# Closing pairs with their first product ahead: B21's transfers issued by GpSimd, three within the product with S4, the fourth behind the first addition

## The chip, the cores and the metric

The kernel runs on one core of a Trainium2 chip. The metric is the device time of one execution in microseconds (us), lower is better. Several executions of a kernel are timed and their median is quoted; one further execution is recorded by the profiler.

The engines are named as in the profile: PE (TensorE, matrix products), PEld (its weight loads), DVE (VectorE), ACT (ScalarE), POOL (GpSimd) and SP (SyncE, which here does nothing but issue transfers). Transfers run on queues of their own; SP, ACT and POOL issue them, each into its own queue.

## The reference

A bidirectional encoder layer on 512 positions of width 2048, all in float32. Cut to what matters here:

```python
h = rmsnorm(x, norm_w)
u = h @ w_in            # z_ssm, xBC, dt, q_a, kv_a, z_attn, g_ssm, g_attn are its column blocks
...                     # branch A: conv, SSD scan in both directions, gated RMSNorm -> y (512 x 2048)
...                     # branch B: latent attention, gated -> o (512 x 2048)
merged = jax.nn.sigmoid(g_ssm) * (y @ w_proj_ssm) + jax.nn.sigmoid(g_attn) * (o @ w_proj_attn)
return rmsnorm(x + merged @ w_out, final_norm_w)
```

The change lies in one product of this, `y @ w_proj_ssm` with its gate: a 512 x 2048 matrix by a 2048 x 2048 one.

## The kernel before

**Products.** A float32 product is made of three passes with rounded parts: every weight chunk of 128 x 1024 is split by `w_split` into a high part (`wh`, an ACT cast, L483) and a low part (`wl`, a DVE subtraction, L484), and PE runs high x high, low x high and high x low (L629, L630, L631). The left operands are split likewise, once each (`split`, the same lines).

**Strassen pairs.** The big products are not made directly: `Strassen.pair(cp)` computes one half of the output columns (cp is 0 or 1) by the Strassen-Winograd scheme, with seven products of quarter size, P1 to P7. Each is made by `product`: four weight chunks m = 0 to 3, each of 12 matmuls of 128 x 512, into two banks. Called A the left matrix and B the right one, the right operands are: B11 for P1, B21 for P2, T1 for P5, T2 = T1 + B22 for P6, B22 for P3, T3 for P7 and, last, T4 for P4, where T4 = T2 + B21. Left operands are x11, x12, x21, x22 and their sums S1 to S4. T1 lies in the tiles X[0] to X[3]; T2 is made in them by `t2`, and T4 by `t4` (L752, a DVE addition of one 128 x 1024 chunk, out X, in X and a raw chunk of B21). B22 lies in the tiles Y; P7's T3 is loaded later, into Y tiles again.

**The closing pairs of w_proj_ssm.** There P1 and P2 of both pairs are made early (`head`), while the attention part runs. So `pair(cp, True)`, run for cp = 0 and then cp = 1, starts with P5 and goes P5, P6, P3 (with S4), P7 (with S3), P4 (with x22). In the pairs that make P2 in their middle, B21 is at hand for `t4` as P2's weights. In the two headed pairs it isn't, and B21 is loaded a second time for T4: `t4_alone` (L754 to L757), called for m = 0 to 3 as P7 takes its chunk m, issues the load on SP's queue (L756) into a tile `wraw` and then the addition. After the pairs of w_proj_ssm come those of w_proj_attn.

**Buffers and hooks.** The tag `wraw` has three buffers of 128 x 1024 in all. In this stage they hold raw halves of left operands (`xraw`, loaded on SP, two for each operand, split later by ACT and DVE) and the B21 chunks of `t4_alone`. Hooks place the work on left operands: at the end of P5 of pair 0, S4 is split and S3 is loaded; at P3's chunk m = 2 (`P3a`), S3 is split and x22 is loaded; at P7's chunk m = 3 (`P7a`), x22 is split. For pair 1 there are others of the kind.

**POOL's queue.** POOL computes nothing here; it issues transfers: loads of gate chunks (`fetch_ps`, L1503, tile `gate`), stores of finished output blocks (`done_ps`, L1513, into `ms_d`), and sums of the next left operands by copies and accumulating copies from DRAM to DRAM (`o_S<-o_x`, `o_S<-o_S`, L1456 and L1459). A transfer that waits holds back those behind it on the issuing engine.

**What sets the order.** PE's order is the order of the code. DVE, ACT, POOL and SP are ordered by a scheduler from priorities; `high_priority(offset=...)` moves an instruction ahead, and `keep_in_program_order` binds it to the order of the code on its engine. Each engine then runs its instructions strictly in that fixed order: an instruction that waits holds those behind it. The scheduler also decides which buffer a tile gets, and with it whose end a load has to wait for.

Of the kernel before, what the change touches and what calls it, by code (L numbers as in the profile page):

```python
# [73 lines left out]
def build(tc, a):  # L74
    nc = tc.nc
    act, dve, pool, pe = nc.scalar, nc.vector, nc.gpsimd, nc.tensor
# [440 lines left out]
    def w_load(t, w, cp, kh, cb, m):  # L517
        with tc.high_priority(offset=LOAD_AHEAD):
            nc.sync.dma_start(t, a[w][cp, kh, cb, m])
        return t  # L520

    def t_load(t, w, cp, name, m, queue=nc.sync):
        with tc.high_priority(offset=LOAD_AHEAD):
            queue.dma_start(t, t_d[w, cp, name][:, m * 1024:(m + 1) * 1024])
        return t
# [27 lines left out]
    def w_more(t, w, cp, kh, cb, m, ahead_=AHEAD):  # L553

        with tc.high_priority(offset=ahead_):
            pool.dma_start(t, a[w][cp, kh, cb, m], accum_op=ALU.add)
# [11 lines left out]
    def col_tile(tag, name, dt=F32):  # L568

        if tag == "Y" and cols is xb:  # L570
            n_cols[0] += 1
            return cols.tile([P, 1024], dt, tag=("Yb", "Ya")[(n_cols[0] - 1) // 2 % 2], bufs=2, name=name)
        return cols.tile([P, 1024], dt, tag=tag, bufs=4, name=name)

    def w_tile(tag):
        with tc.high_priority(offset=LOAD_AHEAD):
            if tag == "w":
                return wp.tile([P, 1024], F32, tag="wraw", bufs=3, name="wraw")
            return col_tile(tag, tag)

    def sum_tile(tag):

        if tag == "kk" or tag == "u" and kk:
            return kk.tile([P, SEQ], F32, tag="kk", bufs=2, name=tag)
        return part_.tile([P, SEQ], F32, tag=tag, bufs=2, name=tag)

    def evict(banks, tag, tile_=None):
        out = []
        with tc.high_priority(offset=AHEAD):
            for i, b in enumerate(banks):  # L590
                out.append(tile_(tag, i) if tile_ else sum_tile(tag))
                act.copy(out[-1], b)
        return out
# [19 lines left out]
    def product(name, op, chunk, extra=None, pre=None):  # L613

        used.append((used[-1] + 1) % 4)
        bs = [b(name) for b in SETS[used[-1]]]
        for m in range(4):
            raw = chunk(m)
            h, l = w_split(raw)
            if extra:  # L620
                extra(m, raw)
            if pre and m == 2:
                pre()
            for i in range(2):
                for jj in range(2):
                    j = 2 * m + jj
                    xh, xl = op(0, j, i), op(1, j, i)
                    wh, wl = (t[:, jj * 512:(jj + 1) * 512] for t in (h, l))
                    pe.matmul(bs[i], xh, wh, start=(j == 0), stop=False)  # L629
                    pe.matmul(bs[i], xh, wl, start=False, stop=False)  # L630
                    pe.matmul(bs[i], xl, wh, start=False, stop=(j == 7))  # L631
                    yield 3
        product_done()
        return bs
# [19 lines left out]
    class Strassen:  # L654
# [60 lines left out]
        def pair(self, cp, headed=False):  # L715
            w, made = self.w, self.made
            X, Y = self.ahead.pop(cp, []), []

            def column(m):
                if m == len(X):  # L720
                    X.append(self.columns(w_tile("X"), cp, m))
                return X[m]

            if headed:
                p1 = self.p1[cp]
            else:
                p1 = evict((yield from product(
                    "P1", self.op("x11"), (lambda m: w_load(w_tile("X"), w, cp, 0, 0, m)) if made else column,
                    None if made else lambda m, raw: w_more(raw, w, cp, 0, 1, m))), "p1", self.tile_)
                self.hook(cp, "P1")  # L730

            def c5(m):
                if m == 1:
                    self.hook(cp, "P5a")
                column(m)
                Y.append(w_load(w_tile("Y"), w, cp, 1, 1, m))
                return X[m]

            T3 = []

            def c7(m):
                if made and not T3:
                    T3.extend(t_load(w_tile("Y"), w, cp, "T3", i) for i in range(4))
                return T3[m] if made else Y[m]

            def t2(m, raw):
                with tc.high_priority(offset=AHEAD):
                    dve.tensor_add(raw, raw, Y[m])

            def t4(m, raw):  # L750
                with tc.high_priority(offset=AHEAD):
                    dve.tensor_add(X[m], X[m], raw)  # L752

            def t4_alone(m, raw):  # L754
                raw = w_tile("w")
                tc.keep_in_program_order(nc.sync.dma_start(raw, a[w][cp, 1, 0, m]))  # L756
                t4(m, raw)  # L757

            p5 = evict((yield from product("P5", self.op("S1"), c5, t2)), "p5", self.tile_)
            self.hook(cp, "P5")  # L760
            A = yield from product("P6", self.op("S2"), lambda m: X[m])
            u = p1 if headed else [self.tile_("u", i) for i in range(2)]
            for i in range(2):
                dve.tensor_add(u[i], p1[i], A[i])
                self.minus_r(p5[i], p5[i], u[i])
            self.hook(cp, "P6")
            if not headed:
                yield from self.second(cp, p1, lambda i: p1[i], t4)
                self.hook(cp, "P2")
            def more(m, raw):  # L770
                if not made:
                    w_more(raw, w, cp, 0, 1, m)
                if m == 2:
                    self.hook(cp, "P3a")

            B = yield from product("P3", self.op("S4"), lambda m: Y[m], more, self.pre(0, 2 * cp + 1))
            for i in range(2):
                o = sum_tile("ms") if headed else self.tile_("C12" if self.last else "p1", i)
                self.r_sum(o, p5[i], B[i])
                self.done(i, 2 * cp + 1, o)  # L780
            self.hook(cp, "P3")
            def late(m, raw):
                if headed:
                    t4_alone(m, raw)
                if m == 3:
                    self.hook(cp, "P7a")

            A = yield from product("P7", self.op("S3"), c7, late, self.pre(2, 2 * cp + 1))
            for i in range(2):
                self.minus_r(p5[i], p5[i], A[i])  # L790
                self.done(2 + i, 2 * cp + 1, p5[i])
                dve.tensor_add(u[i], u[i], A[i])
            self.hook(cp, "P7")
            if self.last:
                yield from self.last("P4", self.op("x22"), lambda m: X[m], u)
                return
            A = yield from product("P4", self.op("x22"), lambda m: X[m], None, self.pre(2, 2 * cp))
            for i in range(2):
                self.r_sum(u[i], u[i], A[i])
                self.done(2 + i, 2 * cp, u[i])  # L800
            self.hook(cp, "P4")
# [1118 lines left out]
```

## Time and profile before

| what | us |
|---|---|
| median of 3 runs (1955.85 to 1956.60) | 1956.28 |
| the profiled execution, its own time | 1956.44 |
| its span | 1954.6 |
| PE busy in the span | 1931.2 |
| DVE busy | 1464.2 |
| ACT busy | 1039.0 |

The span runs from the first to the last instruction of the program; the execution's own time is 1.8 us longer. Times within the span are counted from its start. The stage of the change lies between 1507 and 1621: pair 0 runs P5 from 1506.8, P6 from 1518.0, P3 from 1529.2, P7 from 1540.0 and P4 from 1550.9; pair 1 runs P5 from 1564.4, P6 from 1575.3, P3 from 1586.2, P7 from 1597.1 and P4 from 1609.4; the first product of w_proj_attn starts at 1621.1. The view that compares stretches of time, asked for pair 0, pair 1 and the 56 us behind them, reads (columns: stretch, its length, busy us of each engine with its instructions, granted clock, share of the DMA engines, GB/s):

```profile
1507.00:1564.00 57.00, 54.92 (x239) 44.20 (x238) 50.24 (x53) 27.00 (x28) 7.81 (x14) 1.00 0.80 259
1564.00:1621.00 57.00, 55.54 (x243) 45.15 (x242) 50.68 (x54) 29.45 (x30) 10.98 (x19) 1.00 0.84 282
1621.00:1677.00 56.00, 55.25 (x240) 44.52 (x240) 50.52 (x51) 29.14 (x31) 3.77 (x7) 1.00 0.71 251
```

DVE is busy for 50 of 57 us here, and the DMA engines for 80% and more of the time: nearer to full than in the mean of the kernel.

In the rows of the profile and of the order, names are cut: P is the bank pair of the product that runs, `S__13413` the operand S4, `S__13530` S3, `x__13657` x22, `x__13934` x12 of the attention side, `S__14022` its S1; `p`, `kk`, `ms` are 128 x 512 output blocks.

### The profile page before, as it was taken

What the parts mean: (1) busy time and instruction counts of PE and PEld (TensorE: products, weight loads), DVE (VectorE), ACT (ScalarE), POOL (GpSimd) and SP (SyncE); (2) the same over time, 40 slices, a digit from 0 to 9 for tenths busy, and PEclk for the clock granted to TensorE, in tenths of its full rate; (3) what the DMA queues carried; (4) which work ended last, traced back from release to release, by engine and by line L of the source; (5) the groups of instructions that cost most, each with busy time, mean ns of one, the idle gap of its engine ahead of it and who ended that gap; (6) DMA issues with size and microseconds to landing.
All of it is one profiled execution on the core that took longest, in us unless ns stands there. A gap on an engine that the chain in (4) does not pass through costs nothing.

```text
span 1954.6 us, 24595 instructions
## 1 busy us (share of the span) xinstructions
PE 1931.2 (99%) x8873; PEld 1590.9 (81%) x8874; DVE 1464.2 (75%) x2064; ACT 1039.0 (53%) x1536; POOL 252.8 (13%) x324
## 2 busy tenths in 40 slices
PE   8999999999999999999999999999999999999998
PEld 6878888888888888888888888888888777888886
DVE  7876676766759869789786557676777898879467
ACT  7444444444465866757757444444455455454344
POOL 0011001001112030030210211111011110100011
PEclk9999999999999999999999999999999999999999
DMA  6569669668554545665554867787388887847447
GB/s 219 174 191 260 161 169 248 151 184 242 144 190 153 180 147 158 214 193 179 177 161 147 231 191 208 205 219 201 101 220 303 277 261 279 285 156 243 162 89 170
DMA packets 145306, 383.29 MB, mean 196 GB/s; under 512 B 16608, under 2 KB 34208, under 8 KB 144992
## 3 DMA queue, kind: packets, MB, share of 16 engines
q1 hardware_dynamic: 78240, 232.45, 35.7%
q0 software_dynamic: 31392, 105.40, 23.8%
q10 hardware_dynamic: 35552, 43.87, 6.3%
q8 instruction: 70, 1.15, 0.2%
q14 instruction: 52, 0.43, 0.1%
HBM read 329.55 MB, written 98.17 MB: 219 GB/s over the span
## 4 chain that ended last, share of the span: by engine, by line
PE 48%; DVE 3%; DMA 2%; issue 1%; ACT 0%; SPq 0%; DVEq 0%; ACTq 0%
PE P L630 5%; PE P L631 4%; PE P L629 4%; PE za L169 3%; PE za L171 3%; PE za L170 3%; PE f L1678 1%; PE f L1679 1%; PE f L1680 1%; PE pb L1431 1%; PE qp L171 1%; PE qp L169 1%; PE qp L170 1%; DMA wraw<-wps 1%; DVE wl L484 1%; PE s L1409 1%
## 5 line engine op out<-in xcount | busy, mean ns | idle before, releaser
L483 ACT CAST wh<-X 128x1024 fp32r<-128x1024 f32 x164 | 172.7, 1055 | 198.9 <-PE P L631 156.0
L484 DVE TENSOR_TENSOR wl<-X,wh 128x1024 fp32r<-128x1024 f32 x164 | 199.9, 1223 | 87.0 <-ACT wh L483 86.5
L165 DVE TENSOR_TENSOR wl<-wraw,wh 128x1024 fp32r<-128x1024 f32 (+2 forms) x148 | 173.1, 1172 | 79.8 <-ACT wh L164 74.5
L164 ACT CAST wh<-wraw 128x1024 fp32r<-128x1024 f32 (+2 forms) x148 | 142.8, 969 | 112.6 <-PE za L170 29.0
L484 DVE TENSOR_TENSOR wl<-Y,wh 128x1024 fp32r<-128x1024 f32 x88 | 107.6, 1224 | 71.8 <-ACT wh L483 71.8
L483 ACT CAST wh<-Y 128x1024 fp32r<-128x1024 f32 x88 | 93.0, 1057 | 117.9 <-PE P L631 107.3
L169 PE MATMUL xbc<-h_h,wh 128*128 128x512 f32 x384 | 153.1, 399 | 0.0
L171 PE MATMUL xbc<-h_h,wl 128*128 128x512 f32 x384 | 149.9, 390 | 0.0
L170 PE MATMUL xbc<-h_l,wh 128*128 128x512 f32 x384 | 149.5, 389 | 0.0
L629 PE MATMUL P<-wh,h_h 128*128 128x512 f32 x384 | 149.4, 389 | 0.0
L630 PE MATMUL P<-wl,h_h 128*128 128x512 f32 x384 | 149.4, 389 | 0.0
L631 PE MATMUL P<-wh,h_l 128*128 128x512 f32 x384 | 149.4, 389 | 0.0
L483 ACT CAST wh<-wraw 128x1024 fp32r<-128x1024 f32 x68 | 71.8, 1056 | 115.7 <-PE P L631 63.4
L484 DVE TENSOR_TENSOR wl<-wraw,wh 128x1024 fp32r<-128x1024 f32 x68 | 83.2, 1223 | 60.3 <-ACT wh L483 60.3
L630 PE MATMUL P<-wl,S 128*128 128x512 f32 x288 | 112.4, 390 | 1.4 <-DVE wl L484 1.4
L631 PE MATMUL P<-wh,S 128*128 128x512 f32 x288 | 112.1, 389 | 0.0
L629 PE MATMUL P<-wh,S 128*128 128x512 f32 x288 | 112.1, 389 | 0.0
L169 PE MATMUL za<-h_h,wh 128*128 128x512 f32 x256 | 101.7, 397 | 0.0
L171 PE MATMUL za<-h_h,wl 128*128 128x512 f32 x256 | 100.0, 391 | 0.0
L170 PE MATMUL za<-h_l,wh 128*128 128x512 f32 x256 | 99.7, 389 | 0.0
L171 PEld LDWEIGHTS xbc<-h_h,wl 128*128 128x128 f32 x384 | 72.1, 188 | 15.6
L631 PEld LDWEIGHTS P<-wh,h_l 128*128 128x128 f32 x384 | 72.1, 188 | 15.0
(754 smaller groups left out, 5073.1 us busy)
## 6 DMA issues: line engine op xcount, KB each, us to landing
wraw<-wi SPq DMA_DIRECT2D x102, 512.0 KB, 3.8
T_wps<-wps POOLq DMA_DIRECT2D x32, 512.0 KB, 11.1
da<-da_d SPq DMA_DIRECT2D x64, 256.0 KB, 3.8
T_wpa<-wpa POOLq DMA_DIRECT2D x32, 512.0 KB, 9.7
wraw<-wps SPq DMA_DIRECT2D x24, 512.0 KB, 6.7
wraw<-wo SPq DMA_DIRECT2D x20, 512.0 KB, 3.5
xbc_d<-xbc ACTq DMA_DIRECT2D x24, 256.0 KB, 3.0
wraw<-wun SPq DMA_DIRECT2D x16, 384.0 KB, 6.0
```

Source lines behind the costliest of these rows:

```text
L164: act.copy(h, raw)
L165: dve.tensor_sub(l, raw, h.bitcast(F32))
L169: pe.matmul(out, wh, xh, start=start, stop=False)
L170: pe.matmul(out, wh, xl, start=False, stop=False)
L171: pe.matmul(out, wl, xh, start=False, stop=stop)
L483: i = act.copy(hi_, raw)
L484: dve.tensor_sub(lo_, raw, hi_.bitcast(F32))
L629: pe.matmul(bs[i], xh, wh, start=(j == 0), stop=False)
L630: pe.matmul(bs[i], xh, wl, start=False, stop=False)
L631: pe.matmul(bs[i], xl, wh, start=False, stop=(j == 7))
L1409: pe.matmul(s, qh[:, tk], kh, start=True, stop=False)
L1431: pe.transpose(tp[:, k * P:(k + 1) * P], prs[t][:, k * P:(k + 1) * P], ident)
```

## The change

The load of B21's chunk leaves `t4_alone` and becomes `b21_load`, which takes the next `wraw` tile and issues the load on POOL's queue instead of SP's, in program order there. In the headed pairs it is called three times in P3, at its chunks m = 0, 1 and 2 (at m = 2 ahead of the hook `P3a`), and a fourth time in P7, behind the addition of chunk 0. The additions stay in the code where they were, with priority `AHEAD`. The bytes, the matmuls and the arithmetic are the same. Below the change, lines behind L754 have numbers higher by 7, and those behind L772 by 9 (L1512 is L1521, for one).

```diff
+            b21 = []
+
+            def b21_load():
+                m = len(b21)
+                b21.append(w_tile("w"))
+                tc.keep_in_program_order(pool.dma_start(b21[m], a[w][cp, 1, 0, m]))
+
             def t4_alone(m, raw):
-                raw = w_tile("w")
-                tc.keep_in_program_order(nc.sync.dma_start(raw, a[w][cp, 1, 0, m]))
-                t4(m, raw)
+                t4(m, b21[m])
+                if m == 0:
+                    b21_load()
 ...
             def more(m, raw):
                 if not made:
                     w_more(raw, w, cp, 0, 1, m)
+                if headed and m < 3:
+                    b21_load()
                 if m == 2:
                     self.hook(cp, "P3a")
```

What the scheduler makes of it is seen in the order of the rows on DVE and POOL. First DVE in pair 0, from the end of P6 to the split of S3 (the operand `S__13530`, in the change `S__13536`); the first three `wl<-Y` are the low parts of P3's chunks 0, 1 and 2. Before:

```order
L484 TENSOR_TENSOR S__13413<-xraw,S__13413 128x1024
L484 TENSOR_TENSOR wl<-X,wh 128x1024
L484 TENSOR_TENSOR wl<-Y,wh 128x1024 x2
L764 TENSOR_TENSOR p_13002<-p_13002,P_13422 128x512
L764 TENSOR_TENSOR p_13004<-p_13004,P_13423 128x512
L676 TENSOR_TENSOR p_13409<-p_13409,p_13002 128x512
L484 TENSOR_TENSOR wl<-Y,wh 128x1024
L676 TENSOR_TENSOR p_13411<-p_13411,p_13004 128x512
L484 TENSOR_TENSOR S__13530<-xraw,S__13530 128x1024
```

Now:

```order
L484 TENSOR_TENSOR S__13413<-xraw,S__13413 128x1024
L484 TENSOR_TENSOR wl<-X,wh 128x1024
L484 TENSOR_TENSOR wl<-Y,wh 128x1024
L752 TENSOR_TENSOR X<-X,wraw 128x1024
L484 TENSOR_TENSOR wl<-Y,wh 128x1024
L771 TENSOR_TENSOR p_13002<-p_13002,P_13422 128x512
L771 TENSOR_TENSOR p_13004<-p_13004,P_13423 128x512
L676 TENSOR_TENSOR p_13409<-p_13409,p_13002 128x512
L484 TENSOR_TENSOR wl<-Y,wh 128x1024
L676 TENSOR_TENSOR p_13411<-p_13411,p_13004 128x512
L752 TENSOR_TENSOR X<-X,wraw 128x1024
L484 TENSOR_TENSOR wl<-Y,wh 128x1024
```

The first addition of T4 (L752) now stands ahead of the low part of P3's chunk 1, and the second ahead of that of chunk 3. Before, all four stood behind P3's splits. The third now stands ahead of the low part of P7's chunk 1 and the fourth ahead of that of P4's chunk 1.

The same place in pair 1, DVE, from P3's chunk 2 on; the last `wl<-Y` is P3's chunk 3. Before:

```order
L484 TENSOR_TENSOR wl<-Y,wh 128x1024
L676 TENSOR_TENSOR p_13850<-p_13850,kk 128x512
L676 TENSOR_TENSOR p_13852<-p_13852,kk 128x512
L484 TENSOR_TENSOR wl<-Y,wh 128x1024
L484 TENSOR_TENSOR S__14022<-xraw,S__14022 128x1024 x2
```

Now:

```order
L484 TENSOR_TENSOR wl<-Y,wh 128x1024
L676 TENSOR_TENSOR p_13850<-p_13850,kk 128x512
L676 TENSOR_TENSOR p_13852<-p_13852,kk 128x512
L752 TENSOR_TENSOR X<-X,wraw 128x1024
L484 TENSOR_TENSOR wl<-Y,wh 128x1024
L484 TENSOR_TENSOR S__14028<-xraw,S__14028 128x1024
```

Here the first addition stands ahead of the low part of P3's chunk 3; the second and third stand ahead of those of P7's chunks 1 and 2, the fourth ahead of that of P4's chunk 2.

POOL's queue in pair 0, from the DRAM sums to the stores of the blocks that P3 finishes. Before:

```order
L1459 DMA o_S_223<-o_x_219 128x512
L1459 DMA o_S_221<-o_x_220 128x512
L1503 DMA gate<-gs_d_1_154 128x512
L1513 DMA ms_d_1_178<-ms 128x512
L1503 DMA gate<-gs_d_1_158 128x512
L1513 DMA ms_d_1_182<-ms 128x512
L1503 DMA gate<-gs_d_0_153 128x512
```

Now:

```order
L1468 DMA o_S_223<-o_x_219 128x512
L1468 DMA o_S_221<-o_x_220 128x512
L1512 DMA gate<-gs_d_1_154 128x512
L759 DMA wraw<-wps 128x1024 x3
L1522 DMA ms_d_1_178<-ms 128x512
L1522 DMA ms_d_1_182<-ms 128x512
L759 DMA wraw<-wps 128x1024
L1512 DMA gate<-gs_d_1_158 128x512
L1512 DMA gate<-gs_d_0_153 128x512
```

Three loads stand behind the DRAM sums and a gate load, the fourth behind the stores. In pair 0 the scheduler gives the first load the buffer that the second raw half of S4 leaves, so it waits for that half's split on DVE; the second load gets the buffer of the first and waits for the first addition, the third that of the second and waits for the second addition. In pair 1 the first load stands on POOL behind the accumulating copy `o_S_224<-o_x_218` and waits for the second half of x12 (`x__13934`) to be split on DVE; the second waits for the first addition, the third and fourth get the buffers of S1's raw halves.

## The prediction

> **What bounds the kernel now.** The page's first part says which engine sets the time, and PE's timeline says where it loses any in the stage of the change.
>
> ```profile
> PE 1931.2 (99%) x8873; PEld 1590.9 (81%) x8874; DVE 1464.2 (75%) x2064; ACT 1039.0 (53%) x1536; POOL 252.8 (13%) x324
> ...
> 1534.81 0.39 PE L630 MATMUL P<-wl,S__13413 128*128 128x512 f32 x1
> 1535.04 0.39 PE L631 MATMUL P<-wh,S__13413 128*128 128x512 f32 x1
> ...
> 1556.12 0.39 PE L631 MATMUL P<-wh,x__13657 128*128 128x512 f32 x1
> 1557.26 0.49 PE L629 MATMUL P<-wh,x__13657 128*128 128x512 f32 x1 [0.75 <-ACT wh L483]
> 1559.08 0.50 PE L630 MATMUL P<-wl,x__13657 128*128 128x512 f32 x1 [1.32 <-DVE wl L484]
> 1559.41 0.40 PE L631 MATMUL P<-wh,x__13657 128*128 128x512 f32 x1
> ...
> 1602.50 0.39 PE L629 MATMUL P<-wh,S__13530 128*128 128x512 f32 x1
> 1603.91 0.50 PE L630 MATMUL P<-wl,S__13530 128*128 128x512 f32 x1 [1.02 <-DVE wl L484]
> 1604.25 0.40 PE L631 MATMUL P<-wh,S__13530 128*128 128x512 f32 x1
> ...
> 1609.43 0.39 PE L629 MATMUL P<-wh,x__13657 128*128 128x512 f32 x1
> 1610.25 0.50 PE L630 MATMUL P<-wl,x__13657 128*128 128x512 f32 x1 [0.44 <-DVE wl L484]
> 1610.59 0.39 PE L631 MATMUL P<-wh,x__13657 128*128 128x512 f32 x1
> ```
>
> PE is busy for 99% of the span, so the change can give only what PE waits for. Fed, a matmul starts 0.23 us after the one before (1534.81 to 1535.04); a chunk of 12 takes 2.72. Against that step, P4's chunk 2 in pair 0 loses 1.14 + 1.82 + 0.33 - 3 x 0.23 = 2.6 us. Pair 1 loses 1.41 + 0.34 - 0.46 = 1.3 in P7's chunk 2 and 0.82 + 0.34 - 0.46 = 0.7 in P4's chunk 0, together 2.0. The chain of work that ended last tells what these waited for:
>
> ```profile
> 1535.91 5.61 DMA wraw<-wps
> ...
> 1548.13 6.67 DMA wraw<-wps
> 1554.82 1.23 DVE X L752
> ...
> 1557.89 1.15 DVE wl L484
> ...
> 1592.81 6.93 DMA wraw<-wps
> ```
>
> All of it is B21: the load takes 6.7 us, the addition (L752) follows at once, then ACT's high and DVE's low part. Up to **4.6 us** are at stake in the two pairs. The execution took 1956.44 us, 0.16 above the median of the runs; I add to 1956.4. A measurement tells some 0.2% (3.9 us) from no change, so the whole gain would just be visible.
>
> **What the change moves.** It adds no instruction to PE and leaves DVE's additions at four per pair. The four loads leave SP, whose later loads move up; SP bounds nothing here. What counts is that the loads stand on POOL, and that the additions stand further ahead on DVE, in front of low parts that PE needs sooner. An addition that waits for its load holds the low part behind it. The rows for that, DVE first:
>
> ```profile
> 1522.22 1.23 DVE L484 TENSOR_TENSOR S__13413<-xraw,S__13413 128x1024 fp32r<-128x1024 f32 x1
> ...
> 1527.71 1.23 DVE L484 TENSOR_TENSOR wl<-Y,wh 128x1024 fp32r<-128x1024 f32 x1 [1.50 <-ACT wh L483]
> 1528.86 1.28 DVE L764 TENSOR_TENSOR p<-p,P 128x512 f32<-128x512 f32 x2
> ...
> 1541.54 1.23 DVE L752 TENSOR_TENSOR X<-X,wraw 128x1024 f32<-128x1024 f32 x1 [1.13 <-DMA wraw<-wps]
> 1542.69 1.22 DVE L484 TENSOR_TENSOR wl<-Y,wh 128x1024 fp32r<-128x1024 f32 x1
> ...
> 1557.80 2.36 DVE L484 TENSOR_TENSOR wl<-X,wh 128x1024 fp32r<-128x1024 f32 x2
> ...
> 1585.38 1.23 DVE L484 TENSOR_TENSOR x__13934<-xraw,x__13934 128x1024 fp32r<-128x1024 f32 x1 [1.41 <-ACT x__13934 L483]
> ```
>
> A load that lands at L frees the addition at L + 0.02 (1535.91 + 5.61 = 1541.52, start 1541.54). The low part starts 1.15 later, lasts 1.23, and PE's matmul with it starts 0.06 after (1557.80 + 1.22 = 1559.02, start 1559.08): **L + 2.46**. PE's own times for those matmuls, and the transfers nearest to the new loads (the issues' view, for windows around one or two of them; last column us to landing):
>
> ```profile
> 1532.09 0.39 PE L630 MATMUL P<-wl,S__13413 128*128 128x512 f32 x1
> ...
> 1553.85 0.39 PE L630 MATMUL P<-wl,x__13657 128*128 128x512 f32 x1
> ...
> 1594.57 0.39 PE L630 MATMUL P<-wl,S__13413 128*128 128x512 f32 x1
> ...
> 1523.52 0.33 SPq L495 DMA_DIRECT2D xraw<-yn_x  x1
> xraw<-yn_x SPq DMA_DIRECT2D x1, 512.0 KB, 8.0
> 1520.85 1.25 POOL L1503 DMA_DIRECT2D gate<-gs_d  x1
> o_S<-o_x POOLq DMA_DIRECT2D x1, 256.0 KB, 9.3
> gate<-gs_d POOLq DMA_DIRECT2D x1, 256.0 KB, 9.7
> 1587.65 0.86 POOL L1459 DMA_DIRECT2D o_S<-o_x  x1 [5.88 <-DMA o_S<-o_S]
> Y<-T_wps SPq DMA_DIRECT2D x1, 512.0 KB, 4.4
> o_S<-o_x POOLq DMA_DIRECT2D x1, 256.0 KB, 5.8
> 1542.80 0.33 SPq L756 DMA_DIRECT2D wraw<-wps  x1
> wraw<-wps SPq DMA_DIRECT2D x1, 512.0 KB, 4.0
> wraw<-wpa SPq DMA_DIRECT2D x1, 512.0 KB, 3.2
> ...
> 1546.13 0.55 POOL L1513 DMA_DIRECT2D ms_d<-ms  x1 [0.21 <-issue]
> ```
>
> **Pair 0, first load.** It may be issued when S4's second half is split, 1522.22 + 1.23 = 1523.5. Before, SP issues a load of the same size at that very moment (1523.52), and it takes 8.0, to 1531.5: two DRAM sums are under way. On POOL's queue the load stands behind a gate load that lands at 1520.85 + 9.7 = 1530.6; were it to begin only then, and alone, with 3.2 (the later load of w_proj_attn's weights), it would land at 1533.8. Transfers under way at one time overlap, so I take 1532.2, near the row of the same moment. PE's low pass of P3's chunk 1 then starts at 1532.2 + 2.46 = 1534.7 in place of 1532.09: **2.6 us lost**, from 1.9 to 4.2. Before, that low part was done at 1527.71 + 1.23 = 1528.9, 3.2 us early.
>
> **Pair 0, the rest.** Behind the first addition DVE has the low part of chunk 1 from 1533.4 (1.14 to the next, 2.36 - 1.22), three short sums of 0.6 (1.28 for two with the last one's end), the low part of chunk 2 (1.14), one sum more, and then the second addition. That is reached at 1533.4 + 1.14 + 1.8 + 1.14 + 0.6 = 1538.1, and its load, issued at 1533.4 into the buffer just freed, takes 4.0 to 5.6 (rows of `wraw` above): landed by 1537.4 to 1539.0. The low part of chunk 3 is then 0.3 to 1.2 late; I take 0.3. The third addition, ahead of P7's chunk 1, comes out 0 to 1 late: 0.2. The fourth load stands behind the two stores, which wait for P3's blocks (1546.13 before, some 4 us later now, for the low parts and additions moved ahead of them), and so lands at 1555 to 1557; P4's chunk 1 wants its low part at 1553.85 + 3.1, so L + 2.46 is 0.5 to 2.5 late: 0.8. Together **1.3**, from 0 to 4.5. In return the 2.6 of P4's chunk 2 go: the third addition is then some 10 us earlier than the 1554.82 of before. What is late next is P4's chunk 1, counted here. Pair 0: 2.6 + 1.3 - 2.6 = **+1.3**.
>
> **Pair 1, first load.** It waits for x12's second half (1585.38 + 1.23 = 1586.6), but stands on POOL behind the accumulating copy issued at 1587.65, which lands at 1593.5. A load on SP issued just after that copy took 4.4, to 1592.2: the lower bound. The upper is 1593.5 + 3.2 = 1596.7. I take 1594.6, nearer to the copy's row since that is of its queue. The low part behind the addition is P3's chunk 3, used at 1594.57: 1594.6 + 2.46 - 1594.57 = **2.5 lost**, from 0.1 to 4.6. Pair 0's delay moves both sides alike, because POOL's copies follow stores that wait for DVE.
>
> **Pair 1, the rest, and behind.** The second load follows the first addition (1595.8) and takes 4.0 to 6.9; P7's chunk 1 wants L + 2.46 by 1602.5: 0 to 2.7, I take 0.3. The fourth stands behind the stores again, ahead of P4's chunk 2: 1.0, from 0 to 3. The old losses of 2.0 go. Pair 1: 2.5 + 1.3 - 2.0 = **+1.8**. The loads of w_proj_attn's first chunks follow P4's splits and slip with them: +0.3, from -0.4 to 2.
>
> **Sum.** 1.3 + 1.8 + 0.3 = +3.4, so 1956.4 + 3.4 = **1959.8 us**. All low ends together give -4.6 + 1.9 + 0.1 - 0.4 = -3.0, or 1953.4; all high ends are near +16, but hold only if every transfer is late.
>
> **Rivals.** *It does what it says* (6%): the loads land before DVE comes to the additions, P3 is undisturbed and 4.6 us go: 1951.8. For it the first load of pair 0 has to land by 1532.09 - 2.46 = 1529.6, within 6.1 us of its issue, and that of pair 1 by 1592.1. For it speaks the 3.2 us of a load alone; against it the 8.0, 9.3 and 9.7 of that stretch. The Trainium skill, "DMA: Bandwidth & Descriptors", section "Anatomy of one DMA — SWDGE (gpsimd) path", fits a GpSimd transfer as 2.0 us plus its bytes at 436 GB/s, an estimate of 3.2 us for 512 KB; by that rule this rival would win. The trace differs: the gate load of half that size took 9.7. The same page, section "Queues, rings and completion order", has each DMA engine take the queues in turn and one queue's descriptors in order; by that the load would begin behind the gate load, near the upper bound of 1533.8, and pair 0 would lose some 1.6 us more.
>
> *Only pair 0 is held* (17%): in pair 1 the load overlaps with the copy and lands by 1592.2, and nothing else there is late. Then +1.3 - 2.0 + 0.3 = -0.4: 1956.0.
>
> *The additions form a chain* (25%): one buffer serves the first three loads of pair 0, so each is issued only after the addition before it. If each then takes 6 to 7 us, as B21's loads did in the rows of the chain, every addition holds its low part: pair 0 loses 4.2 + 4.0 - 2.6, pair 1 4.0 + 2.5 - 2.0, and w_proj_attn's start 1: near +11; with half of the terms late, +8. It decides where a load takes over 5 us on POOL. Against it speak the 4.0 us of the load at 1542.80 and the loads that the stalled DVE doesn't free yet, which leave the queues emptier. 1964.5 as its middle. This one is clearly slower.
>
> **How the numbers follow.** Forecast 52%, with its own range of 1957.5 to 1962; the rivals 6, 17 and 25. The range of 1955.0 to 1965.5 takes in the second rival and most of the chain and leaves out the first. Slower by over 0.2% (past 1960.2) is most of the chain and some two fifths of the forecast: 0.45. Within 0.2%: the rest of the forecast and all of the second rival, 0.5. Faster: 0.05.
>
> **What would show it.** In the profile after: the waits of PE at 1557.26, 1559.08, 1603.91 and 1610.25 are gone; DVE idles ahead of L752, released by `DMA wraw<-wps`, twice within P3, near 1532 and 1595, for 2 to 5 us; PE waits for `wl` at L630 with `S__13413` right behind. The `wraw` transfers of POOL take 5 to 9 us for each pair's first, 4 to 6 for the others. If PE has no wait with `S__13413`, the forecast is wrong and the first rival holds; if waits stand at three or more chunks of a pair with over 1 us each, it is the chain.

## The result, and the profile after

| | median of the runs | profiled execution | its span |
|---|---|---|---|
| before | 1955.85 us (5 runs, 1954.21 to 1956.60) | 1956.44 us | 1954.6 us |
| after | 1968.39 us (5 runs, 1967.62 to 1970.75) | 1968.39 us | 1966.6 us |

The ratio is 1.0068, with a 95% interval of 1.0056 to 1.0079: the change makes the kernel slower by 12.5 us. The forecast was 1959.8, its range ended at 1965.5. The side was right, the size was not.

PE's timeline of the changed kernel, at the six places where it loses time in the two pairs (a row: start, duration, engine, line, what it does, and in brackets the idle time with what ended it):

```profile
1530.46 0.39 PE L629 MATMUL P<-wh,S__13413 128*128 128x512 f32 x1
1533.17 0.71 PE L630 MATMUL P<-wl,S__13413 128*128 128x512 f32 x1 [2.33 <-DVE wl L484]
1533.68 0.63 PE L631 MATMUL P<-wh,S__13413 128*128 128x512 f32 x1
1534.11 0.63 PE L629 MATMUL P<-wh,S__13413 128*128 128x512 f32 x1
...
1547.03 0.50 PE L630 MATMUL P<-wl,S__13536 128*128 128x512 f32 x1 [1.07 <-DVE wl L484]
...
1557.82 0.39 PE L629 MATMUL P<-wh,x__13657 128*128 128x512 f32 x1
1561.01 0.80 PE L630 MATMUL P<-wl,x__13657 128*128 128x512 f32 x1 [2.80 <-DVE wl L484]
1561.60 0.63 PE L631 MATMUL P<-wh,x__13657 128*128 128x512 f32 x1
...
1602.12 0.50 PE L630 MATMUL P<-wl,S__13413 128*128 128x512 f32 x1 [1.36 <-DVE wl L484]
...
1611.60 0.50 PE L630 MATMUL P<-wl,S__13536 128*128 128x512 f32 x1 [0.72 <-DVE wl L484]
...
1622.43 0.39 PE L629 MATMUL P<-wh,x__13657 128*128 128x512 f32 x1
1626.96 0.80 PE L630 MATMUL P<-wl,x__13657 128*128 128x512 f32 x1 [4.14 <-DVE wl L484]
```

All six waits are for a low part. A wait is counted here as the step from one start to the next less the 0.23 us of a fed matmul: 2.5, 1.2, 3.0, 1.5, 0.9 and 4.3 us, together 13.4. Of the four places at which PE lost time before, three have no loss now. At the fourth, P7's chunk 2 in pair 1 (1603.91 before, 1611.60 now), PE still loses 0.9 us, now behind the third addition. Behind the 2.5 us wait something stands that the profile before has behind none of its waits: the matmuls last 0.63 instead of 0.39 and start 0.43 apart (1533.68 to 1534.11). The same holds behind the two waits in P4.

The first of the waits on DVE's timeline, what DVE waited for in the whole stretch (the view of waits: total, times, longest), and the chain of work that ended last in the second pair:

```profile
1523.58 1.23 DVE L484 TENSOR_TENSOR wl<-Y,wh 128x1024 fp32r<-128x1024 f32 x1 [0.45 <-ACT wh L483]
1530.76 1.23 DVE L752 TENSOR_TENSOR X<-X,wraw 128x1024 f32<-128x1024 f32 x1 [5.95 <-DMA wraw<-wps]
1531.90 1.22 DVE L484 TENSOR_TENSOR wl<-Y,wh 128x1024 fp32r<-128x1024 f32 x1
```

```profile
DVE X L752 <- DMA wraw<-wps: 22.2, 6, 6.6
```

```profile
1603.50 5.66 DMA wraw<-wps
...
1612.74 1.13 DVE wl L484
1613.88 0.61 DVE ms L1521
...
1615.99 8.53 DMA wraw<-wps
1624.54 1.23 DVE X L752
1625.77 1.15 DVE wl L484
1626.96 0.80 PE P L630
```

Both show the predicted mechanism: the load lands, the addition that DVE stood waiting at follows at once, then the low part behind it, then PE. The load that does most harm is the fourth. It is issued at 1615.99, behind a store that waited for the sum at 1613.88, and then takes 8.5 us.

The mean granted clock (PEclk) of stretches of 3.41 us, cut where the halved clock begins and ends in the trace (columns: the stretch, its length, busy time of PE, of its weight loads, of DVE, ACT and POOL with their instructions, PEclk, share of the DMA engines, GB/s):

```profile
1529.88:1533.29 3.41, 1.08 (x6) 0.58 (x5) 2.53 (x3) 1.95 (x3) 0.53 (x1) 1.00 0.11 44
1533.29:1536.70 3.41, 3.41 (x9) 2.64 (x10) 3.41 (x6) 0.00 (x0) 0.00 (x0) 0.50 0.89 294
1557.19:1560.60 3.41, 1.01 (x5) 0.51 (x3) 2.01 (x2) 0.68 (x1) 0.00 (x0) 1.00 0.98 382
1560.60:1564.01 3.41, 3.00 (x7) 2.43 (x8) 3.41 (x6) 0.37 (x1) 0.00 (x0) 0.50 1.00 359
1622.04:1625.45 3.41, 0.78 (x4) 0.32 (x2) 0.91 (x1) 0.00 (x0) 0.00 (x0) 1.00 1.03 420
1625.45:1628.87 3.42, 1.91 (x5) 1.53 (x6) 3.42 (x6) 2.00 (x2) 0.10 (x1) 0.50 0.92 340
```

A stretch in which PE does little is followed by one at half speed. It costs 25 matmuls about 0.2 us each (4.9 us), and 0.7 at the first steps behind the waits: 5.6 us.

### The profile page after: what moved, and what is told of

It is laid out like the page before. It is cut to its first block, busy times and chain, and to the rows that moved or that the text cites. A ratio compares the mean times of both kernels' runs of the same rounds, so it can differ in the third digit from the quotient of the medians.

```text
span 1966.6 us, 24608 instructions
## 1 busy us (share of the span) xinstructions
PE 1935.5 (98%) x8874; PEld 1595.3 (81%) x8874; DVE 1461.3 (74%) x2064; ACT 1037.4 (53%) x1536; POOL 256.5 (13%) x332
```

## The experiments

The theory at this point: **the additions' place** on DVE, in front of low parts, makes PE wait for whatever load is late; the fourth load is late because of its place on POOL; the half clock is a result of the waits. The main rival: GpSimd's queue is itself slow. A ratio is always to the kernel before, run beside it on the same chip.

**Other queue, other place of the additions, fourth load alone.** Three kernels, each the change with one edit:

```diff
 # x1_sp
-tc.keep_in_program_order(pool.dma_start(b21[m], a[w][cp, 1, 0, m]))
+tc.keep_in_program_order(nc.sync.dma_start(b21[m], a[w][cp, 1, 0, m]))
 # x2_add_behind
-t4(m, b21[m])
+tc.keep_in_program_order(dve.tensor_add(X[m], X[m], b21[m]))
 # x3_fourth_sp
-tc.keep_in_program_order(pool.dma_start(b21[m], a[w][cp, 1, 0, m]))
+tc.keep_in_program_order((nc.sync if m == 3 else pool).dma_start(b21[m], a[w][cp, 1, 0, m]))
```

> The four loads of B21 are called at the places of the change, but go through SP's queue; the additions stand on DVE where the change has them (one of them a low part further ahead). Theory 'place of the additions' (the loads get their buffers late and the additions hold low parts, whatever queue carries them): PE still waits with S4's operand in P3 and P4, in all 8 us or more, and the time stays at 1963 to 1970. Rival 'POOL's queue' (it is GpSimd's transfers, behind gate loads and stores, that are slow): the loads take 3 to 5 us, no wait of PE in the two pairs is over 1.5 us, and the time is 1951 to 1957.

> The loads are those of the change, on POOL, but the four additions are held on DVE behind the low parts of the chunk of P7 in whose place they stand in the code, so that in P3 no low part stands behind an addition. Theory 'place of the additions': the waits of PE in P3 (2.49 and 1.52 us) go, and with the first the half clock behind it; what is left is P4's, the time 1955 to 1962. Rival 'POOL's queue': the loads are as late as before, now ahead of P7's and P4's low parts, and PE waits there for as much: 1964 to 1970.

> Only the fourth load of each pair goes through SP's queue, at the same place of the program; the first three stay on POOL, with the additions in front of low parts. If the fourth load's place behind POOL's stores is the dearest part (2.96 and 4.30 us of waits in P4 and 3.4 us of half clock behind them in the change), those go: 1956 to 1961, with P3's 2.5 and 1.5 left. If the buffer that the fourth load waits for, or the memory traffic of that stretch, makes it late, P4's waits stay at 2 us or more and the time at 1964 to 1970.

| | median, us | ratio (95%) | what PE still waits for |
|---|---|---|---|
| x1 | 1958.52 | 1.001 (1.0001 to 1.002) | P3 2.2; nothing else over 1.03 |
| x2 | 1955.15 | 0.9993 (0.9984 to 1.0003) | P4 0.8, 1.2 and 1.3 |
| x3 | 1962.78 | 1.003 (1.002 to 1.004) | P3 2.5 and 2.9; P7 0.9 twice; P4 1.2 and 0.5 |

x1 lies between the two expectations, and its parts tell why. Its first load is issued at 1522.38 and takes 8.3 us on SP, where GpSimd's took 8.2 from 1522.58 in the change: for this load the queue makes no difference, and a wait of 2.2 us in P3 stays. What SP does better is where other loads stand. The fourth starts at 1547.75 instead of 1551.34, since it stands behind no store. Pair 1's first load starts ahead of the accumulating copy and not behind it; it takes 5.2 us instead of 6.8, and P3's wait of 1.5 us there is gone. x2 keeps every load on POOL and is no slower than the kernel before: with the additions behind the low parts the whole 12.5 us are back. What PE still waits for there is this:

```profile
1553.25 0.50 PE L629 MATMUL P<-wh,x__13657 128*128 128x512 f32 x1 [0.62 <-ACT wh L483]
1554.70 0.50 PE L630 MATMUL P<-wl,x__13657 128*128 128x512 f32 x1 [0.95 <-DVE wl L484]
...
1611.23 0.50 PE L630 MATMUL P<-wl,x__13657 128*128 128x512 f32 x1 [1.13 <-DVE wl L484]
```

Its fourth loads still stand behind the stores and still take 7.3 and 7.6 us, but with DVE undisturbed they are issued sooner, at 1545.90 and 1601.18 instead of 1551.34 and 1615.99. x3 takes the fourth load alone to SP, and P4's waits fall from 3.0 and 4.3 to 1.2 and 0.5; P3 still waits twice, 2.5 and 2.9 us where it was 2.5 and 1.5. So both parts are real: without the additions' place nothing measurable is lost, and with it the stores ahead of the fourth load make the largest waits.

x3 held a surprise. Its waits of 2.5 and 2.9 us in P3 left the clock at full speed, where 2.5 us in the change had halved it.

**How long a wait halves the clock.** In the kernel before, DVE repeats some low parts:

```diff
             split_into(h, l, raw)
+            for _ in range(LONGER.get(n_split[0], 0)):   # 3 to 9, one chunk in 12
+                dve.tensor_sub(l, raw, h.bitcast(F32))
```

> The kernel before, in which DVE repeats the low part of one chunk in every 12, from the 60th on, 3 to 9 times (twice over), with the same result, so that PE waits for it for lengths between 0 and some 8 us, far from the two pairs. Theory 'a long wait halves the clock': behind each wait of over some 2.5 us PE's rows show the granted clock at half for 3.4 us or a multiple of it, and matmuls 0.43 us apart, and behind none under 1.8 us. Rival 'something in the last pairs' (the transfers or the load of the chip there): waits as long elsewhere leave the clock at full.

It did, far from the two pairs (one execution, 2089.28 us). PE had 13 long waits at the repeated low parts: the two of 1.7 us left the clock at 1.00, the eleven of 4.0 to 17.9 us all led to half speed. The shortest of these, at 304.78 us of the span, with the stretch ahead and the two behind:

```profile
301.76:305.17 3.41, 0.39 (x2) 0.35 (x3) 3.41 (x4) 1.36 (x2) 1.74 (x3) 1.00 0.57 89
305.17:308.58 3.41, 3.41 (x10) 2.64 (x9) 0.75 (x2) 1.23 (x2) 0.70 (x1) 0.50 1.07 208
308.58:312.00 3.42, 3.42 (x17) 2.83 (x16) 1.23 (x1) 1.05 (x1) 0.21 (x1) 1.00 1.02 217
```

The half speed lasts 3.41 us behind this wait of 4.0 us; with the wait of 17.9 us it lasts 20.48, and begins before that wait ends. All its beginnings and ends in one trace lie on one grid of 3.41 us. So the clock is a matter of the wait alone, not of the last pairs; whether length or place in the grid decides was left for the next run.

**The same kernel again** (no edit):

> The changed kernel once more, nothing edited. In the runs so far the halved stretches of clock begin on a grid of 3.41 us, and a window of it in which PE was idle for 2.4 us or more is followed by half speed, one with at most 1.94 us is not; waits of 2.51 and 2.85 us that a border of the grid cut in two left the clock at full. Theory 'grid': where the borders fall is another matter in each execution, so in this profile the waits of some 2.5 and 3.0 us may or may not be followed by half speed, each as its part within one window says, the wait of 4.3 us is always, and the executions differ by up to some 3 us, the shorter with the higher mean clock. Rival 'length alone': each wait of 2.49 us or more is followed by half speed again, whatever its place in the grid, and the times agree within 1 us.

Median 1968.90 us, ratio 1.0065 (1.0050 to 1.0080), 4 runs from 1966.93 to 1969.10. In this profile the wait of P3 is again 2.5 us, from 1530.5 to 1533.0, but a border of the grid (1531.48) cuts it:

```profile
1528.07:1531.48 3.41, 2.57 (x12) 1.80 (x10) 0.90 (x1) 3.41 (x4) 0.00 (x0) 1.00 0.54 220
1531.48:1534.89 3.41, 1.90 (x8) 1.58 (x9) 3.41 (x6) 0.15 (x1) 0.53 (x1) 1.00 0.44 129
1534.89:1538.30 3.41, 3.41 (x16) 2.56 (x15) 3.41 (x4) 1.05 (x1) 0.39 (x1) 1.00 0.84 285
...
1609.98:1613.39 3.41, 1.66 (x7) 1.40 (x8) 3.41 (x5) 0.45 (x1) 0.00 (x0) 1.00 0.20 66
1613.39:1616.80 3.41, 3.41 (x16) 2.80 (x16) 3.41 (x5) 1.06 (x1) 1.78 (x4) 1.00 0.68 237
1623.64:1627.05 3.41, 0.25 (x1) 0.25 (x2) 2.66 (x3) 1.33 (x2) 0.00 (x0) 1.00 1.03 419
1627.05:1630.46 3.41, 3.41 (x9) 2.65 (x9) 3.41 (x6) 2.67 (x3) 1.08 (x2) 0.50 0.98 338
```

The clock stays full behind it, and behind a wait of 2.3 us in P7 (PE busy 1.66 of that stretch). It falls behind the two waits in P4, 3.8 and 4.0 us here. The grid theory holds; "length alone" falls. By the grid, a wait of 2.5 us halves the clock in one execution and not in the next.

**The low part last in PE's chunk.** If PE asks for `wl` later, the waits should shrink. Three kernels with another order of the 12 matmuls in P3, P7 and P4 of the pairs, on the change (x6), on the kernel before (x7) and on x2 (x8), in short:

```diff
-for i, jj: xh*wh, xh*wl, xl*wh
+for i, jj: xh*wh;  for i, jj: xl*wh;  for i, jj: xh*wl
```

> The change, with PE's 12 matmuls of a chunk in another order in P3, P7 and P4 of the two pairs: the four products of the high parts, then the four with the operand's low part, then the four that need the chunk's low part `wl`. PE then asks for `wl` seven matmuls later, 7 x 0.227 = 1.6 us, and the scheduler puts each addition one place further back. Theory 'PE waits for low parts held behind late additions': every wait shrinks by at least 1.6 us, those of 1.5 us and less go, hardly any halved clock is left, 1953 to 1959. Rival 'DVE as a whole is behind' (its lost time is only handed on, and PE waits for the next chunk instead): 1963 to 1969.

> The kernel before with the same other order of PE's matmuls in P3, P7 and P4 of the two pairs. Its 4.6 us of waits are for `wl` behind late additions, 1.6 us at most each (1.1 of them for a high part): with `wl` asked for 1.6 us later, 1951 to 1954. Rival: the later `wl` brings the next chunk's high part or the loads behind it late, nothing is won, 1955 to 1958.

> Both together: the change's loads on POOL, the additions held behind the low parts of P7's chunks, and the low part last in PE's chunks. What was left of waits in the run with the additions behind (0.78, 1.23 and 1.29 us in P4, 0.6 in the next projection) should go: 1951 to 1953, faster than both kernels. Rival: POOL's loads come so late that P4's chunks wait for more than 1.6 us all the same: 1954 to 1957.

None is faster: 1967.46 us (ratio 1.0059, 1.0042 to 1.0076), 1957.10 (1.0008, 0.9998 to 1.0017) and 1959.45 (1.0019, 1.0010 to 1.0029). x6 and x7 end where their rivals had them. x8 is slower than both its ranges: P4 waits 1.2 and 1.4 us, P5 of pair 1 waits 1.9, and w_proj_attn three times 1.0 to 1.3. In x6 P3 waits 1.8, P7 1.8 and 0.7, P4 3.0 and 5.9. The last is a wait for a **high** part, since a late addition delays the chunk of X itself:

```profile
1626.08 1.23 DVE L756 TENSOR_TENSOR X<-X,wraw 128x1024 f32<-128x1024 f32 x1 [7.89 <-DMA wraw<-wps]
```

```profile
1627.41 1.04 ACT L483 CAST wh<-X 128x1024 fp32r<-128x1024 f32 x1 [12.60 <-DVE X L756]
```

This edit is no clean one: the scheduler also set additions and loads elsewhere for it. It shows that 1.6 us of slack at the low part don't cure lateness of X, no more. x7 adds one thing on the clock: two waits of 2.0 and 1.2 us within one stretch of the grid halved it like one long wait.

**One cause at a time.** x9 holds only the first addition behind the low parts; x10 calls the fourth load in P3 with the others, ahead of the stores; x11 has no addition on DVE at all:

```diff
 # x9_first_behind, in t4_alone
-t4(m, b21[m])
+if m == 0:
+    tc.keep_in_program_order(dve.tensor_add(X[m], X[m], b21[m]))
+else:
+    t4(m, b21[m])
 if m == 0:
     b21_load()
 # x10_fourth_ahead, in t4_alone and in P3
-if m == 0:
-    b21_load()
...
-if headed and m < 3:
+if headed:
     b21_load()
 # x11_accum, in P3, and t4_alone is gone
-if headed and m < 3:
-    b21_load()
+if headed:
+    tc.keep_in_program_order(pool.dma_start(X[m], a[w][cp, 1, 0, m], accum_op=ALU.add))
```

> Of the change only the first addition of each pair is held behind the low parts that are before it in the code; the other three keep their priority, and all four loads stay on POOL where the change has them (the fourth is issued behind the first addition, as before). Theory 'each wait has its own cause': P3's waits (2.49 and 1.52 us) and the half clock behind the first go, P4's (3 to 4 us, with their half clock) stay: 1962 to 1965. Rival 'the delay of P3 makes the later ones': with P3 undisturbed the stores are earlier, the fourth load too, and nothing over 1.5 us is left: 1954 to 1958.

> The fourth load is called in P3 with the other three, and so stands on POOL ahead of the two stores of P3's blocks; nothing else of the change is edited. Theory 'behind the stores' (they wait for P3's blocks, and the load starts at 1551 amid the transfers that follow): the load starts some 6 us earlier, as it did on SP, P4's waits are 1.3 us or less, 1958 to 1964. Rival 'a load on GpSimd's queue is slow by itself there': P4 still waits 2.5 us or more, 1965 to 1970.

> No load of B21 and no addition on DVE: in P3, POOL issues for each of the four chunks a transfer from memory that adds B21 onto X on its way, as other sums of this kernel are made. Theory 'what costs is the addition in DVE's order': with no addition DVE holds no low part, the transfers (5.8 to 9.3 us each) are done before P4 splits X, the waits of PE in P3, P7 and P4 are gone: 1951 to 1954, faster than both kernels. Rival: the adding transfers wait for one another or take over 10 us, P4's high parts wait for X: 1956 to 1962.

x9: 1962.62 us (1.0031, 1.0018 to 1.0044). P3 has no wait, P7 waits 1.3 and 2.1, P4 still 2.9 and 4.7, each of these two with half clock behind it. x10: 1962.65 us (1.0036, 1.0023 to 1.0049). P4's waits are 0 and 0.6; P3 waits 2.3 and 2.9, P7 1.1 and 2.1. In pair 0 the fourth load starts at 1545.81 and takes 4.0 us; in the change it took 7.2 from 1551.34. In pair 1 it starts 13 us sooner (1602.94 against 1615.99) and takes 7.0 instead of 8.5. Both did as the theory says, and either edit is worth about 6 us of the 12.5. What surrounds the fourth load is seen in the stretches of its two transfers in the change and, in the last row, of pair 0's in x10:

```profile
1551.34:1558.57 7.23, 6.86 (x31) 5.35 (x29) 3.71 (x4) 2.11 (x2) 1.60 (x4) 1.00 0.93 354
1616.00:1624.50 8.50, 6.82 (x31) 5.30 (x29) 1.95 (x3) 1.06 (x1) 2.66 (x5) 1.00 0.94 364
...
1545.81:1549.84 4.03, 3.14 (x14) 2.56 (x15) 3.77 (x5) 2.93 (x4) 0.53 (x1) 1.00 0.97 358
```

The DMA engines are busy for 93 and 94% in the change, but for 97% in x10 too, so their share does not tell a slow load from a fast one. The number of transfers does. In the change the sums that release the stores also release two gate loads behind them, and SP's loads run at the same time: in pair 0 three transfers are under way when the fourth load is issued, and six more are issued before it lands; in x10 it is three and two. That this company makes the load slow fits these numbers, but no run varied it alone.

x11 took 1957.27 us (1.0009, 0.9999 to 1.0019), within its rival's range of 1956 to 1962. P3 has no wait, but P7 now waits three times in each pair, 0.3 to 1.0 us a time. The adding transfers land about 4 us apart (1533.7, 1537.5, 1541.3, 1545.1), 13 to 20 us behind their issue, and other loads share the way with them.

**Can the loads win anything?** Three more versions were meant to beat both kernels. x12 calls all four loads in P3 and holds the additions behind the low parts of P3's chunk 3 and P7's 0, 1 and 2; x13 calls the fourth load right behind the third; x14 makes the fourth an adding transfer:

```diff
 # x12_all_early, in t4_alone, in P3 and in P7
-t4(m, b21[m])
-if m == 0:
-    b21_load()
+tc.keep_in_program_order(dve.tensor_add(X[m], X[m], b21[m]))
...
-if headed and m < 3:
+if headed:
+    if m == 3:
+        t4_alone(0, None)
     b21_load()
...
-if headed:
-    t4_alone(m, raw)
+if headed and m < 3:
+    t4_alone(m + 1, raw)
 # x13_fourth_buffer: at m == 2 b21_load() twice, at m == 3 only t4_alone(0, None)
 # x14_fourth_accum: at m == 3 pool.dma_start(X[3], a[w][cp, 1, 0, 3], accum_op=ALU.add) and t4_alone(0, None)
```

> Meant to beat both: all four loads of B21 are called in P3 and stand on POOL ahead of the stores, the first addition is held on DVE behind the low part of P3's last chunk and the other three behind those of P7's chunks 0, 1 and 2, so that an addition stands in front of low parts only where its load has had 7 us or more. Theory: P3 has no wait, and the waits that the run with the additions behind had left in P4 (0.78, 1.23 and 1.29 us, for the fourth load) go as well: 1951.5 to 1953.5, ratio below 0.999. Rival 'the memory traffic': the fourth load, or the loads of SP that follow, only come late elsewhere, and the next products wait instead: 1954.5 to 1957.

> As x12, but the fourth load is called right behind the third, in P3's chunk 2: in both pairs it then stands on POOL ahead of the stores, and in the first pair it takes the buffer that the first addition frees near 1536 and not the third's near 1545. Theory 'place and buffer': it lands by 1545, the one wait that x12 had left (3.46 us, and 1.8 of half clock behind it) goes, no wait of PE over 0.7 us in the two pairs: 1950.5 to 1953, ratio 0.9975 to 0.999. Rival 'traffic': SP's loads, or the third load, are late for it, and PE waits 2 us or more in P7 or P4: 1954 to 1957.

> As x12, but the fourth chunk of B21 is added onto X by POOL's transfer itself, called in P3's last chunk: it needs no buffer and no addition on DVE. Theory 'place and buffer': it starts near 1533, takes 6 to 10 us among the others, and is done before P4 needs X: 1950.5 to 1953. Rival 'traffic': an adding transfer (4 us each in a row in x11) puts off the loads behind it, and PE waits for them: 1954 to 1958.

x12: 1955.61 us (1.0002, 0.9993 to 1.0011). Pair 1 has no wait at all. In pair 0 the scheduler set the fourth load behind the stores all the same, and it waited for the buffer of the third addition; PE waits 3.5 us, with half clock. x13 mends that: all four loads land by 1543.45. It takes 1956.39 us (1.0004, 0.9995 to 1.0013), because the wait has moved. SP's queue, then ACT, then PE in P4's third chunk (m = 2) of pair 0:

```profile
1547.48 0.33 SPq L495 DMA_DIRECT2D xraw<-yn_x  x1
```

```profile
1555.60 1.05 ACT L483 CAST x__13657<-xraw 128x1024 fp32r<-128x1024 f32 x1 [6.79 <-DMA xraw<-yn_x]
```

```profile
1557.64 0.49 PE L629 MATMUL P<-wh,x__13657 128*128 128x512 f32 x1 [1.41 <-ACT wh L483]
1559.09 0.77 PE L630 MATMUL P<-wl,x__13657 128*128 128x512 f32 x1 [0.96 <-DVE wl L484]
```

The second raw half of P4's own operand x22 shares the three `wraw` buffers with B21. In the change it is issued at 1542.36; here it has to wait until the last additions give a buffer back, and so comes 5 us later. x14 took 1958.37 us (1.0016, 1.0007 to 1.0025): in pair 1 a load issued behind the adding transfer takes 12.5 us, and PE waits 5.8 for its low part. x12 and x13 ended in their rivals' ranges, x14 0.4 us above its own; in x12 and x13 the cause, though, is the order and the buffer, not the traffic that the rivals named. Of all versions none is faster than the kernel before beyond what these runs can tell; x2, at 0.9993, is its equal.

## Why the prediction was wrong

**What bounds the kernel** and **the mechanism** were right. PE waits for low parts behind additions that wait for B21, at L + 2.46: the first load lands at 1530.73 and PE starts at 1533.17, 2.44 later. Three of the four old losses went; the table counts the other one, P7's chunk 2 of pair 1, as gone (in the -2.0) and as new (in the +0.9). DVE waited twice within P3 as announced (5.95 us at 1530.76, 2.43 at 1599.71), and at four more additions. x2 and x9 show the mechanism by taking the additions away from the low parts. The terms of the sum, in us:

| term | predicted | measured |
|---|---|---|
| pair 0, first load | +2.6 | +2.5 |
| pair 0, second and third | +0.5 | +1.2 |
| pair 0, fourth | +0.8 | +3.0 |
| pair 0, old loss | -2.6 | -2.6 |
| pair 1, first load | +2.5 | +1.5 |
| pair 1, second and third | +0.3 | +0.9 |
| pair 1, fourth | +1.0 | +4.3 |
| pair 1, old loss | -2.0 | -2.0 |
| start of w_proj_attn | +0.3 | -1.8 |
| half clock behind long waits | none | +5.6 |
| sum | +3.4 | +12.6 |

The execution after is 11.95 us longer than that before. PE was also ready for P3's low pass 1.4 us sooner than before (1530.46 + 0.23 against 1532.09), and 1.1 us of this lead stand already some 136 us into the span, far ahead of the change. So 12.6 less 1.4 leaves 0.75 unexplained, small steps spread over the stretch. Pair 0's first load also landed 1.5 us sooner than forecast, so its lateness came out right. In pair 1 the copy that the forecast reckoned from is issued at 1587.65 in both profiles: pair 0's delay did not move both sides alike. Of the terms "second and third", all that was measured is the third's; in pair 1 it stands ahead of P7's chunk 2, and the sum had no term for that.

**The step that failed most is the fourth load** ("lands at 1555 to 1557", "0.5 to 2.5 late: 0.8"). Its place, behind the stores, and the store's delay of 4 us were right (1546.13 before, 1550.20 after). Its duration was taken from the 4.0 and 5.6 us of `wraw` rows, and it took 7.2 in pair 0 (landing at 1558.57) and 8.5 in pair 1, amid what the same event set free. The trace before spoke against the short rows: B21's eight loads there took 6.7 us in the median, and those of the change 6.6. The view of the issuing line, before and after:

```profile
DMA to landing us min/median/max: 4.0/6.7/7.4
...
DMA to landing us min/median/max: 4.1/6.6/8.5
```

Within its ranges the sum also took low values, 0.8 of 0.5 to 2.5 and 1.0 of 0 to 3; the waits of 3.0 and 4.3 lie above both ranges. x10 and x3 show the price of that place. The two terms are off by 5.5 us.

**The step that was missing is the clock.** All waits were priced at their length. The three waits of 2.5 us and more cost over half as much again, 5.6 us on their 9.8. The trace before shows this behind no wait, since its longest is 1.7 us, but the sum had terms of 2.6, and matmuls of the slow length do stand in that trace: PE's first ten, up to 5.2 us of the span (shortest, median and longest, in ns):

```profile
L267 PE MATMUL dtp<-idle x10: 517/634/634, 1.4 to 5.2; 128*128 128x512 bf16 x10
```

The Trainium skill, "TensorE: Matmul & The Clock Gate", Part 1 on the clock gate, describes this halving and a free-running window of 3413 ns. The trace agrees with the window; the same page of the Trainium skill takes an idle window of about 3.4 us for the condition, where 1.9 us of idle time within one were enough here (PE busy 1.48 of 3.42 us in x12, rows at the end).

**The start of w_proj_attn** came out on the other side: the 0.4, 0.7 and 0.7 us that PE lost there with three operands vanished. That PE, some 12 us later, finds operands ready whose loads did not slip as far is argued, not shown.

**The rivals.** "The additions form a chain" came nearest: more than half of the loads late, and 8 to 11 us. It was given 25% and the condition that "a load takes over 5 us on POOL", which six of the eight loads fulfilled (4.1 to 8.5 us). By the prediction's own sign, waits of over 1 us at three or more chunks of a pair, pair 0 is the chain (2.5, 1.2 and 3.0); pair 1 has two such waits. The link through one buffer held too: the second and third loads of pair 0 were issued only behind the addition before. Its +11 comes near the measured 12.5 partly by luck, since it had no half clock either. "It does what it says" needed the first load by 1529.6; it landed at 1530.73. Nor did the load begin only behind the gate load ahead of it on POOL: that one landed at 1529.2, 1.5 us earlier, while no such load took under 3.2 us in any run, and on SP the load of the same place took 8.3 us.

That no other order of this change brings the gain is shown for the versions tried (x8, x11 to x14), not for all.

## What to carry to other kernels

A prefetch can cost its whole lateness when work that is due sooner is queued behind the instruction that consumes it: before an operand is loaded earlier, look at where its consumer lands on its engine, and pin the consumer behind the work that is due sooner. Price a transfer by the rows of its own place and by the transfers that the same event releases, not by the shortest equal one, and ask whose buffer it takes. And a wait that leaves TensorE idle for some 2 us within 3.4 may cost more than its length.

## What the hardware showed that was not expected

- The clock that PE is granted falls to 0.50 in steps of 3.41 us on a grid that runs on by itself: its phase differed between executions of the same kernel. Stretches with PE busy for 1.48 us or less were followed by half speed; with 1.65 (the kernel before, from 1944.21), 1.66 (x5, above) or more they were not, in all sixteen profiles. The border lies between. In x12 (the rows below) a wait of 3.5 us is cut in two by the grid: the first stretch keeps 2.04 us of work and leaves the clock full, the second keeps 1.48 and halves it.

```profile
1552.76:1556.17 3.41, 2.04 (x10) 1.35 (x8) 1.08 (x1) 0.00 (x0) 0.00 (x0) 1.00 1.03 413
1556.17:1559.59 3.42, 1.48 (x6) 1.23 (x7) 3.42 (x6) 1.99 (x2) 0.64 (x2) 1.00 0.49 162
1559.59:1563.00 3.41, 3.41 (x9) 2.64 (x8) 3.41 (x5) 1.03 (x1) 0.95 (x2) 0.50 0.95 288
```

- Once halved, the clock comes back only behind a stretch that is nearly full: in the change the stretch from 1625.45, idle for its first 1.5 us, was followed by another at half speed; behind the one from 1560.60, idle for 0.4 us, it was full again. In x14 a half-speed stretch with PE busy for 2.8 us (from 1599.66) was still followed by another, so the border lies between that and the 3.0 of the stretch from 1560.60.
- A 512 KB load took the same time through GpSimd's queue as through SP's when issued at nearly the same moment (8.2 and 8.3 us, one load in each of two kernels), while four transfers that add onto X came one behind the other, 4 us apart.
